# Splitting the loads of three early units into shares of partitions, in an instance norm on one core

## The chip, the core and the metric

The kernel runs on one core of one Trainium2 chip. The metric is the device time of one execution in microseconds (us). Before the change the median of three runs is 626.89 us (626.75 to 627.43). The core has five engines: TensorE (PE), VectorE (DVE), ScalarE (ACT), GpSimd (POOL) and SyncE (SP). Data moves between the main memory (HBM) and the on-chip memory (SBUF, 128 partitions) by 16 DMA engines. SP, ACT and POOL can start a transfer; SP and ACT each have a queue of their own, which the profile calls q1 (SP) and q10 (ACT). POOL's is q0.

## The reference

```
B, G, C_per_g, H, W = 4, 8, 16, 256, 256        # x, float32; gamma is (G, C_per_g)
mu  = x.mean(axis=(3, 4), keepdims=True)
var = ((x - mu) ** 2).mean(axis=(3, 4), keepdims=True)
out = (x - mu) / np.sqrt(var + 1e-5) * gamma[None, :, :, None, None]
```

For each of 4 x 8 x 16 = 512 images of 256 x 256 values the kernel takes the mean and the variance, normalizes, and multiplies by one factor per channel. Everything is float32. Each value has to be read once and written once: 134.2 MB in and 134.2 MB out.

## The kernel before, in words

**Tiling.** One image of 65,536 values is laid over S = 8 partitions, 8,192 values (32 KB) on each. So 16 images fill 128 partitions: this is a *unit*, 4 MB, and there are 32 units, numbered u = 0 to 31. Both `xv[u]` and `ov[u]` are 128 rows of 32 KB that lie one behind the other in HBM; row p of a unit goes to partition p. Partition p holds part p % 8 of image p // 8.

**Buffers.** Six SBUF buffers `slots[0..5]` (tiles `xt0` to `xt5`, in the profile `xt`), used in turn: unit u has slot u % 6. The normalization works in place, the store reads the slot, and the load of unit u + 6 can start when the store of unit u has landed.

**The order of the work** is the order in which the program is written (`manual_schedule`); the framework adds the waits. At the start, ahead of all computing:

- DVE clears a small tile `touch`, and POOL writes it (16 rows of 512 bytes) over the heads of every eighth row of unit 0 of the output (L54). The first store waits for that write. POOL also loads gamma (L55).
- Units 0 to 5 are loaded (L56, L57 through `load`, L47, L48): units 1 and 3 from ACT's queue, units 0, 2, 4 and 5 from SP's. Each is one transfer of 128 rows.
- L59 and L60 write 60 no-ops for ACT.
- Constants are made, among them the matrix `navg` that averages over the 8 partitions of an image, and gamma is brought to one value per partition (L83 to L94). ACT's first computing work is L78, a square root that needs its function table loaded.

Then one round for each unit u:

1. DVE sums each row of the slot (L107); beside it ACT squares it and sums the squares (L108, output thrown away).
2. TensorE multiplies the two sums by `navg` (L116); the result is minus the mean and minus the mean square.
3. DVE makes minus the variance (L117), ACT takes the root (L121), DVE the reciprocal (L125) and the product with gamma (L127).
4. DVE normalizes the slot in place (L130).
5. ACT issues the store (L134). SP issues the load of unit u + 6 (L136).

**Queues.** A queue works its transfers off in the order of issue. From unit 0 on, all stores are on ACT's queue (q10) and all further loads on SP's (q1). ACT and SP are in-order: an issue that has to wait holds up what stands behind it on that engine.

**Completion semaphores.** The transfers of SP and ACT share eight completion semaphores (numbers 99, 101, 112, 113, 114, 116, 117 and 118 in the trace). The framework deals them out in turn. An issue that gets a semaphore whose last transfer has not been seen to land waits for it first. In the program before, the six first loads and the first two stores use up the eight, so no load at the start waits.

Of the kernel before, what the change touches and what calls it, by code (L numbers as in the profile page):

```python
# [1 line left out]

# [4 lines left out]

F32 = mybir.dt.float32
U8 = mybir.dt.uint8
ALU = mybir.AluOpType  # L10
ACTF = mybir.ActivationFunctionType
AX = mybir.AxisListType


@with_exitstack
def kernel(
    ctx: ExitStack,
    tc: tile.TileContext,
    x: bass.AP,
    gamma: bass.AP,  # L20
    out: bass.AP,
):
    nc = tc.nc
    B, G, C, H, W = x.shape
    P = nc.NUM_PARTITIONS
    HW = H * W
    n_ch = B * G * C
    S = 8
    K = P // S
    F = HW // S  # L30
    U = n_ch // K
    NG = (G * C) // K
    AHEAD = 6
    assert HW % S == 0 and (G * C) % K == 0

    xv = x.rearrange("b g c h w -> (b g c h w)").rearrange("(u p f) -> u p f", p=P, f=F)
    ov = out.rearrange("b g c h w -> (b g c h w)").rearrange("(u p f) -> u p f", p=P, f=F)
    gv = gamma.rearrange("g c -> (g c)")

    data = ctx.enter_context(tc.tile_pool(name="data", bufs=1))  # L40
    singles = ctx.enter_context(tc.tile_pool(name="singles", bufs=1))
    psum = ctx.enter_context(tc.tile_pool(name="psum", bufs=4, space=bass.MemoryType.PSUM))
    ctx.enter_context(tc.manual_schedule())

    slots = [data.tile([P, F], F32, name=f"xt{i}") for i in range(AHEAD)]

    def load(u, queue):  # L47
        queue.dma_start(out=slots[u % AHEAD][:], in_=xv[u])  # L48


    g_row = singles.tile([1, G * C], F32, name="g_row")
    touch = singles.tile([16, 128], F32, name="touch")
    nc.vector.memset(touch[:], 0.0)  # L53
    nc.gpsimd.dma_start(out=ov[0][0::S, 0:128], in_=touch[:])  # L54
    nc.gpsimd.dma_start(out=g_row[:], in_=gv[None, :])  # L55
    for u in range(AHEAD):  # L56
        load(u, nc.scalar if u in (1, 3) else nc.sync)  # L57

    for _ in range(60):  # L59
        nc.scalar.nop()  # L60

    eps_t = singles.tile([P, 1], F32, name="eps_t")
    nc.gpsimd.memset(eps_t[:], 1e-5)
    one = singles.tile([1, 1], F32, name="one")
    nc.gpsimd.memset(one[:], 1.0)
    navg = singles.tile([P, K, S], F32, name="navg")
    nc.gpsimd.memset(navg[:], -1.0 / HW)  # L67
    nc.gpsimd.affine_select(  # L68
        out=navg[:], in_=navg[:], pattern=[[-S, K], [0, S]], compare_op=ALU.is_ge,
        fill=0.0, base=0, channel_multiplier=1,  # L70
    )
    nc.gpsimd.affine_select(  # L72
        out=navg[:], in_=navg[:], pattern=[[S, K], [0, S]], compare_op=ALU.is_ge,
        fill=0.0, base=S - 1, channel_multiplier=-1,
    )
    navg_w = navg[:].rearrange("p k s -> p (k s)")
    root_eps = singles.tile([P, 1], F32, name="root_eps")
    nc.scalar.activation(out=root_eps[:], in_=eps_t[:], func=ACTF.Sqrt)  # L78
    g_rep = singles.tile([1, NG, K, S], F32, name="g_rep")
    g_ps = psum.tile([P, NG], F32, name="g_ps", bufs=1)  # L80
    g_col = singles.tile([P, NG], F32, name="g_col")

    nc.vector.tensor_copy(  # L83
        out=g_rep[:],
        in_=g_row[:].rearrange("o (n k) -> o n k", n=NG).unsqueeze(3).to_broadcast([1, NG, K, S]),
    )
    for n in range(NG):
        nc.tensor.matmul(  # L88
            out=g_ps[:, n : n + 1],
            lhsT=g_rep[:, n].rearrange("o k s -> o (k s)"),  # L90
            rhs=one[:],
            start=True, stop=True,
        )
    nc.vector.tensor_copy(out=g_col[:], in_=g_ps[:])  # L94

    junk = singles.tile([P, F], U8, name="junk")

    st = singles.tile([P, U, 2], F32, name="st")
    nvar = singles.tile([P, U], F32, name="nvar")
    std = singles.tile([P, U], F32, name="std")  # L100
    rstd = singles.tile([P, U], F32, name="rstd")
    scale = singles.tile([P, U], F32, name="scale")

    squares = []
    for u in range(U):
        t = slots[u % AHEAD]
        nc.vector.reduce_sum(out=st[:, u, 0:1], in_=t[:], axis=AX.X)  # L107
        square = nc.scalar.activation(  # L108
            out=junk[:], in_=t[:], func=ACTF.Square, accum_out=st[:, u, 1:2],
        )  # L110
        if u:

            tc.declare_no_dep(square.ins, squares[-1].ins, reason="junk, ordered by the root between")
        squares.append(square)
        ps = psum.tile([P, 2], F32, name="ps")
        nc.tensor.matmul(out=ps[:], lhsT=navg_w, rhs=st[:, u], start=True, stop=True)  # L116
        nc.vector.tensor_scalar(  # L117
            out=nvar[:, u : u + 1], in0=ps[:, 0:1], scalar1=ps[:, 0:1],
            scalar2=ps[:, 1:2], op0=ALU.mult, op1=ALU.add,
        )  # L120
        nc.scalar.activation(  # L121
            out=std[:, u : u + 1], in_=nvar[:, u : u + 1], func=ACTF.Sqrt,
            bias=eps_t[:], scale=-1.0,
        )
        nc.vector.reciprocal(out=rstd[:, u : u + 1], in_=std[:, u : u + 1])  # L125
        g = u % NG
        nc.vector.tensor_mul(  # L127
            out=scale[:, u : u + 1], in0=rstd[:, u : u + 1], in1=g_col[:, g : g + 1],
        )
        nc.vector.tensor_scalar(  # L130
            out=t[:], in0=t[:], scalar1=ps[:, 0:1], scalar2=scale[:, u : u + 1],
            op0=ALU.add, op1=ALU.mult,
        )
        nc.scalar.dma_start(out=ov[u], in_=t[:])  # L134
        if u + AHEAD < U:
            load(u + AHEAD, nc.sync)  # L136


# [1 line left out]
_INS = ['x', 'gamma']  # L140
_OUTS = [((4, 8, 16, 256, 256), 'float32')]


# [23 lines left out]
```

## Time and profile before

| What | Value | From |
|---|---|---|
| time, median of 3 runs | 626.89 us (626.75 to 627.43) | runs |
| span of the profiled execution, its own time from the first to the last instruction | 624.9 us | page, head |
| DVE, ACT, PE, POOL busy | 443.4, 238.8, 21.4, 2.4 us | page, part 1 |
| bytes moved, mean rate over the span | 268.46 MB, 430 GB/s | page, part 2 |
| one load or store of a unit | 4096 KB | page, part 6 |
| from issue to landing, median: stores, SP's loads, ACT's two loads | 62.5, 38.5, 31.5 us | page, part 6 |
| row sum of a unit (DVE), squares (ACT), normalization (DVE) | 8685, 7030, 4550 ns | page, part 5 |
| instructions recorded on ACT | 98 | page, part 1 |

The page belongs to one profiled execution. The runs are timed without a profile; their median is 2.0 us above the span, which leaves that much around the first and the last instruction. In the page, part 2 cuts the span into 40 equal slices of 15.62 us; a digit is the busy share in tenths. The rate row below it says what the 16 DMA engines together moved in each slice.

Besides the page, the trace holds one record for every packet of every transfer: its queue, start, duration and size. A packet here is one row of 32,768 bytes; a packet of 4 bytes is the signal to a completion semaphore, one per DMA engine and transfer. There are 8,192 packets of 32,768 bytes: 512 for each of the 16 DMA engines.

### The profile page before, as it was taken

The page shows a single profiled execution, that of the slowest core. Times are in us where ns is not written, and L with a number is a line of the kernel's source. Part 1 is how long each engine was busy: PE and PEld are TensorE (multiplying, and loading weights), DVE is VectorE, ACT ScalarE, POOL GpSimd, SP SyncE. Part 2 cuts the span into 40 slices and gives each one's busy share as a digit, 9 for nine tenths or more (in the row PEclk, how much of TensorE's full clock was granted, in tenths as well). Part 3 has the DMA queues.
Part 4 walks back from the last instruction along what each step waited for, and adds up shares of the span by engine and source line. Part 5 has one row for each costly group of instructions (what it writes and reads, how often), then busy time and mean ns, then how long its engine had stood idle before and what let it go on. Part 6 is the DMA issues. An engine that isn't in the chain of part 4 may idle for free.

```text
span 624.9 us, 631 instructions
## 1 busy us (share of the span) xinstructions
PE 21.4 (3%) x80; PEld 19.5 (3%) x80; DVE 443.4 (71%) x163; ACT 238.8 (38%) x98; POOL 2.4 (0%) x11
## 2 busy tenths in 40 slices
PE   0200000000000000000000000000000000000000
PEld 0200000000000000000000000000000000000000
DVE  0588999999776687666786767867668676687730
ACT  0444444444443234432344423444224442244400
POOL 1000000000000000000000000000000000000000
DMA  8999999999999999999999999999999999999998
GB/s 370 436 426 430 422 434 436 436 436 437 432 424 433 436 436 424 436 436 434 436 436 432 422 436 436 434 426 436 436 434 436 436 434 419 436 436 434 426 436 369
DMA packets 9282, 268.46 MB, mean 430 GB/s; under 512 B 1072, under 2 KB 1088, under 8 KB 1088
## 3 DMA queue, kind: packets, MB, share of 16 engines
q10 hardware_dynamic: 4896, 142.61, 52.9%
q1 hardware_dynamic: 4320, 125.83, 46.8%
q0 software_dynamic: 64, 0.01, 0.0%
q14 instruction: 2, 0.02, 0.0%
HBM read 134.22 MB, written 134.23 MB: 430 GB/s over the span
## 4 chain that ended last, share of the span: by engine, by line
another core or an unknown queue 61%; DMA 17%; DVE 15%; SPq 1%; PE 1%; issue 0%; ACT 0%
DVE st L107 10%; DMA xt<-in_x_dram 10%; DMA out_dram<-xt 8%; DVE xt L130 5%; SPq L48 1%; PE ps L116 1%; ACT std L121 0%; DVE nvar L117 0%; DVE rstd L125 0%; DVE scale L127 0%
## 5 line engine op out<-in xcount | busy, mean ns | idle before, releaser
L107 DVE TENSOR_REDUCE st<-xt 128x1 f32<-128x8192 f32 x32 | 277.9, 8685 | 100.4 <-DMA xt<-in_x_dram 100.4
L108 ACT ACTIVATE junk<-xt 128x8192 uint8<-128x8192 f32 x32 | 225.0, 7030 | 275.1 <-DMA xt<-in_x_dram 231.9
L130 DVE TENSOR_SCALAR xt<-xt,ps,scale 128x8192 f32<-128x8192 f32 x32 | 145.6, 4550 | 1.2
L121 ACT ACTIVATE std<-nvar,eps_t 128x1 f32<-128x1 f32 x32 | 9.4, 294 | 79.6 <-DVE nvar L117 79.6
L116 PE MATMUL ps<-st,navg 128*128 128x2 f32 x64 | 17.9, 349 | 557.1 <-DVE st L107 557.1
L116 PEld LDWEIGHTS ps<-st,navg 128*128 128x128 f32 x64 | 16.0, 311 | 558.9 <-issue 558.9
L117 DVE TENSOR_SCALAR nvar<-ps 128x1 f32<-128x1 f32 x32 | 9.2, 287 | 23.8 <-PE ps L116 23.8
L125 DVE RECIPROCAL rstd<-std 128x1 f32<-128x1 f32 x32 | 5.2, 164 | 11.6 <-ACT std L121 11.6
L83 DVE COPY g_rep<-g_row 1x1024 f32<-1x1024 f32 x1 | 0.7, 681 | 14.3 <-DMA g_row<-in_gamma_dram 14.3
L108 ACT ACTIVATION_READ_ACCUMULATOR junk<-xt 128x1 f32 x32 | 6.0, 186 | 0.0
L127 DVE TENSOR_TENSOR scale<-rstd,g_col 128x1 f32<-128x1 f32 x32 | 5.1, 159 | 1.1
L88 PE MATMUL g_ps<-one,g_rep 1*128 1x1 f32 x16 | 3.5, 347 | 16.1 <-DVE g_rep L83 16.1
L88 PEld LDWEIGHTS g_ps<-one,g_rep 1*128 1x128 f32 x16 | 3.5, 325 | 16.1 <-issue 16.1
L94 DVE COPY g_col<-g_ps 128x8 f32<-128x8 f32 x1 | 0.2, 166 | 3.7 <-PE g_ps L88 3.7
L78 ACT ACT_TABLE_LOAD x1 | 1.3, 1283 | 1.7 <-PEq L151 1.7
L53 DVE MEMSET touch<- 16x128 f32 x1 | 0.2, 165 | 0.9 <-PEq L151 0.9
L54 POOL DMA_DIRECT2D out_dram<-touch x1 | 0.6, 619 | 0.8 <-DVE touch L53 0.8
L55 POOL DMA_DIRECT2D g_row<-in_gamma_dram x1 | 0.5, 487 | 0.0
L68 POOL TENSOR_SCALAR_AFFINE_SELECT navg<-navg 128x128 f32<-128x128 f32 x1 | 0.4, 400 | 0.1
L72 POOL TENSOR_SCALAR_AFFINE_SELECT navg<-navg 128x128 f32<-128x128 f32 x1 | 0.4, 399 | 0.1
L67 POOL MEMSET navg<- 128x128 f32 x1 | 0.2, 232 | 0.0
L78 ACT ACTIVATE root_eps<-eps_t 128x1 f32<-128x1 f32 x1 | 0.2, 203 | 0.0
(6 smaller groups left out, 0.6 us busy)
## 6 DMA issues: line engine op xcount, KB each, us to landing
out_dram<-xt ACTq DMA_DIRECT2D x32, 4096.0 KB, 62.5
xt<-in_x_dram SPq DMA_DIRECT2D x30, 4096.0 KB, 38.5
xt<-in_x_dram ACTq DMA_DIRECT2D x2, 4096.0 KB, 31.5
out_dram<-touch POOLq DMA_DIRECT2D x1, 8.0 KB, 9.1
g_row<-in_gamma_dram POOLq DMA_DIRECT2D x1, 0.5 KB, 13.3
```

Source lines behind the costliest of these rows:

```text
L48: queue.dma_start(out=slots[u % AHEAD][:], in_=xv[u])
L78: nc.scalar.activation(out=root_eps[:], in_=eps_t[:], func=ACTF.Sqrt)
L83: nc.vector.tensor_copy(out=g_rep[:], in_=g_row[:].rearrange("o (n k) -> o n k", n=NG).unsqueeze(3).to_broadcast([1, NG, K, S]),)
L88: nc.tensor.matmul(out=g_ps[:, n : n + 1], lhsT=g_rep[:, n].rearrange("o k s -> o (k s)"), rhs=one[:], start=True, stop=True,)
L107: nc.vector.reduce_sum(out=st[:, u, 0:1], in_=t[:], axis=AX.X)
L108: square = nc.scalar.activation(out=junk[:], in_=t[:], func=ACTF.Square, accum_out=st[:, u, 1:2],)
L116: nc.tensor.matmul(out=ps[:], lhsT=navg_w, rhs=st[:, u], start=True, stop=True)
L117: nc.vector.tensor_scalar(out=nvar[:, u : u + 1], in0=ps[:, 0:1], scalar1=ps[:, 0:1], scalar2=ps[:, 1:2], op0=ALU.mult, op1=ALU.add,)
L121: nc.scalar.activation(out=std[:, u : u + 1], in_=nvar[:, u : u + 1], func=ACTF.Sqrt, bias=eps_t[:], scale=-1.0,)
L125: nc.vector.reciprocal(out=rstd[:, u : u + 1], in_=std[:, u : u + 1])
L127: nc.vector.tensor_mul(out=scale[:, u : u + 1], in0=rstd[:, u : u + 1], in1=g_col[:, g : g + 1],)
L130: nc.vector.tensor_scalar(out=t[:], in0=t[:], scalar1=ps[:, 0:1], scalar2=scale[:, u : u + 1], op0=ALU.add, op1=ALU.mult,)
```

## The change

`load` cuts the first use of three slots into several transfers. A share is written as (first, step): partitions first, first + step, first + 2 step and so on, with the rows of the unit in HBM that belong to them.

- Units 2 and 3: (0, 8) and (4, 8) with 16 rows each, (2, 4) with 32 rows, (1, 2) with 64 rows.
- Unit 4: (0, 4) and (2, 4) with 32 rows each, (1, 2) with 64 rows.
- All other units stay one transfer of 128 rows. The 64 large transfers become 72.
- The loop of 60 no-ops is taken out of the source.

```
+    shares = {
+        2: ((0, S), (S // 2, S), (S // 4, S // 2), (1, 2)),
+        3: ((0, S), (S // 2, S), (S // 4, S // 2), (1, 2)),
+        4: ((0, S // 2), (S // 4, S // 2), (1, 2)),
+    }
+
     def load(u, queue):
-        queue.dma_start(out=slots[u % AHEAD][:], in_=xv[u])
+        for first, step in shares.get(u, ((0, 1),)):
+            queue.dma_start(out=slots[u % AHEAD][first::step], in_=xv[u][first::step])
...
     for u in range(AHEAD):
         load(u, nc.scalar if u in (1, 3) else nc.sync)
-
-    for _ in range(60):
-        nc.scalar.nop()
```

With more transfers at the start, the eight completion semaphores come round sooner, and the built program has waits at these issues that it did not have before:

- SP: the fourth share of unit 2 waits until unit 0 has landed; the three shares of unit 4 wait for the first share of unit 3 and the first and second of unit 2; unit 5 waits for the third share of unit 3.
- ACT: the fourth share of unit 3 waits until unit 1 has landed. ACT's function table (L78 before, L83 after) stands behind it.
- The stores of units 0, 1 and 2 wait for the second share of unit 3, the third of unit 2 and the first of unit 4; the stores of units 4 and 5 for the loads of units 5 and 6.

From unit 6 on, the transfers are the same as before and in the same order; the semaphores fall back into the old rotation.

## The prediction, made before the changed kernel was run

> **What bounds the kernel now.** I read the page's head and parts 2 and 3 first, to see which resource is full.
>
> ```profile
> span 624.9 us, 631 instructions
> ...
> DMA  8999999999999999999999999999999999999998
> GB/s 370 436 426 430 422 434 436 436 436 437 432 424 433 436 436 424 436 436 434 436 436 432 422 436 436 434 426 436 436 434 436 436 434 419 436 436 434 426 436 369
> DMA packets 9282, 268.46 MB, mean 430 GB/s; under 512 B 1072, under 2 KB 1088, under 8 KB 1088
> ...
> q10 hardware_dynamic: 4896, 142.61, 52.9%
> q1 hardware_dynamic: 4320, 125.83, 46.8%
> ```
>
> The DMA engines are busy in every slice, and the rate stops at 436 to 437 GB/s. The two queues together take 99.7% of the engines' span. So the compute engines matter only if they leave the queues without work. Then the chain of waits, in the steady part:
>
> ```profile
> 159.95 18.96 another core or an unknown queue
> 178.91 0.02 SPq L48
> 178.93 0.03 issue
> 178.96 0.33 SPq L48
> 179.29 18.95 another core or an unknown queue
> 198.25 0.02 SPq L48
> ```
>
> SP issues one load per 198.25 - 178.91 = 19.34 us, each time a store has landed. In that time each DMA engine moves 8 rows of a load and 8 of a store: 19.34 / 16 = 1.21 us per row. The trace's packet records say the same: 98% of the 8,192 rows take 1.213 us, none under 1.211, on both queues alike. The floor is then 512 x 1.213 = 621.06 us of rows per engine. The first row starts at 1.80 us and the last signal is at 623.61; the floor would end at 622.86. Only 0.75 us are lost over the whole kernel, and 1.3 us follow.
>
> How much room have the waits? The timeline of the start:
>
> ```profile
> 0.80 0.88 ACTq L48 DMA_DIRECT2D xt<-in_x_dram  x2
> ...
> 1.72 1.28 ACT L78 ACT_TABLE_LOAD   x1 [1.72 <-PEq L151]
> ...
> 3.01 0.20 ACT L78 ACTIVATE root_eps<-eps_t 128x1 f32<-128x1 f32 x1
> ...
> 22.62 7.03 ACT L108 ACTIVATE junk<-xt 128x8192 uint8<-128x8192 f32 x1 [19.41 <-DMA xt<-in_x_dram]
> 22.62 8.69 DVE L107 TENSOR_REDUCE st<-xt 128x1 f32<-128x8192 f32 x1 [2.73 <-DMA xt<-in_x_dram]
> 29.56 0.19 ACT L108 ACTIVATION_READ_ACCUMULATOR junk<-xt 128x1 f32 x1
> 31.42 0.50 PEld L116 LDWEIGHTS ps<-st,navg 128*128 128x128 f32 x2 [11.82 <-issue]
> ...
> 37.68 0.35 ACTq L134 DMA_DIRECT2D out_dram<-xt  x1
> ```
>
> ACT's issues end at 1.68 and its table load starts at 1.72: the 60 no-ops take no time between them and the trace has no record of one. Units 0 and 1 land at 22.25 (records), units 2 and 3 at 41.7; store 0 is issued 3.6 us ahead of that (41.26, when the first engine turns to it).
>
> **The change, part by part.**
>
> *No-ops.* Nothing on the chip goes away: 0 us.
>
> *More signals.* Eight more transfers put eight more 4-byte packets on each DMA engine. In the records one takes 0.009 us, and the next packet starts 6 ns later: 8 x 0.006 to 0.009 = 0.05 to 0.07 us. I take 0.05. All of it is on the path, for nothing covers the full resource. The rows themselves stay 512 per engine if a share of 16 rows gives one to each engine; the 16 rows of `touch` did so (16 records that start between 7.12 and 7.69, one behind a row of each engine).
>
> *ACT's new wait.* ACT sits until unit 1 has landed, wakes at 22.62 (as its squares did), issues the fourth share of unit 3 (0.4, from 0.88 for 2), loads its table (1.28) and takes L78's root (0.20). The squares of unit 0 begin at about 24.5, not 22.62, and end at 31.5, READ_ACCUMULATOR at 31.75. TensorE started at 31.42, just after DVE's sum. Unit 0 and its store come 0.4 us later: 38.1. Cover: units 2 and 3 keep the engines until 41.26, 3 us to spare. DVE carries the 0.4 on to unit 8 (its round of 14.93 us gains on the 19.34 of the loads until then), always with a store waiting in the queue. Cost 0; if the cover were gone, 0.4.
>
> *SP's new waits.* The fourth share of unit 2 is issued at 22.6 and needed at 21.7 + 8 rows x 1.213 = 31.4 (four rows of each queue go ahead). Unit 4 then waits for shares that land by 31, unit 5 for unit 3's third share, by 31 to 37; they are needed at 41 and 61. The next in SP, load 6, waits for store 0 (61.8) as now. Room 8 us or more each: 0.
>
> *The stores' new waits.* Store 0 waits for a share that lands by 27 (ready 38), store 1 by 37 (ready 53), store 2 by 52 (ready 68), stores 4 and 5 for loads 5 and 6, at about 81 and 100 (ready 98 and 113). Each is done 10 us early or more, and still 5 us early if the loads come 4.85 later: 0.
>
> *The shares of 16 rows.* No row of this trace prices them: every large transfer in it has 128 rows. Each engine gets four rows of this kind (two first shares, two second shares). Below: 0, each stays at 1.213; a gain is excluded by the 1.211 minimum. Above: two engines meet at the same part of SBUF and share one engine's rate, 2 x 1.213 per row, 4 x 1.213 = +4.85 us. Which? The row time is 1.213 where both queues load (units 2 and 3, 22 to 38 us) and where loads run beside stores (from 44 us on), for reading HBM and for writing it. Such a ceiling belongs to the DMA engine or to its way into SBUF. A whole load has all 128 partitions, so no engine need meet another; a share (0, 8) uses every eighth partition only, and if neighbours share a way, some ways get two engines and others none. The second share uses the idle ones, but a queue comes to it only later, and units 2 and 3 go through the same shares side by side, so the other queue gives no relief. I take the upper end, less a little: two engines out of step by s do not meet for s at each end. The starts of the 16 engines lie 0.57 us apart (21.67 to 22.24), and the closest pair sets the end: s about 0.1, 0.2 off. +4.65 us.
>
> The Trainium skill, page "SBUF — State Buffer", section "Door 1: The DMA port swizzle", gives a map by which partitions 0, 8, 16 ... 120 reach eight of 16 ports, two rows each, and 4, 12 ... 124 the other eight; it puts a port at one engine's rate, so a 16-row share would go at half speed: an estimate of +4.85 for the term, against 0 if the rows stay at the trace's 1.213. No run here shows it yet.
>
> *The shares of 32 and 64 rows.* Below 0, above 1.213 more on each of the other 20 rows per engine (2 + 4 of unit 2, 2 + 4 of unit 3, 2 + 2 + 4 of unit 4): +24.3. I take 0: step 4 and step 2 still touch every group of four neighbours, as a whole load does, with two and four rows per engine.
>
> **Sum.** 0.05 + 0 + 4.65 = 4.7 us. The profiled execution's span goes from 624.9 to 629.6; with the 2.0 us around it (626.89 - 624.9) the time is 631.6. Nothing gives it back, since the rows run to the end: the last store is issued at 600.3 and then waits in the queue until 623.6.
>
> **Rivals.**
>
> *The limit is in the engine, not on the way into SBUF* (not slower). Place: the first two shares of units 2 and 3, 21.7 to 31.4. It decides if a way carries two engines at once; then only the signals are left: 626.9 + 0.05 = 626.9. For it: each DMA engine alone explains the 1.213. Against it: nothing in the trace, which never makes two engines meet. Chance 0.26, the small shifts by instruction fetches (two records of 8 KB at 155.6 and 199.1, 0.3 us each on one engine) within it.
>
> *The wide shares collide too*, all 24 split rows of an engine: 626.9 + 4.85 + 24.3 = 656. It needs rows of a wide share to be dealt out otherwise than in a whole load. Chance 0.04.
>
> *A queue runs dry behind a wait* that lands late, which needs 3 us (store 0) or 8 us (the loads) more than worked out, on both queues at once. It would cost a few us on top: 634 to 637. Chance 0.03.
>
> *Faster.* What is lost now is 0.75 us, so 626.1 at best; over 0.2% (1.25 us) faster needs what the floor excludes. 0.02, for an error in my reading.
>
> **How the numbers follow.** The likeliest case has 0.65: 631.6, its own range 630.5 to 632.3 (from pairs 0.5 us out of step, 626.9 + 3.9 with 0.3 of noise off, to 626.9 + 4.85 + 0.07 with 0.5 of noise on; the runs spread 0.68). For 8 in 10 the engine rival must be inside: 626.4 to 632.4, leaving out 656, the dry queue and the faster case. 0.2% is 1.25 us, about what a measurement of this kernel tells from no change. Slower 0.65 + 0.04 + 0.03 = 0.72, the same 0.26, faster 0.02.
>
> **What would show it.** In the records of units 2 and 3: 64 rows of about 2.4 us on 16 engines between 21.7 and 31.4 and nowhere else; the rate row's slices 2 and 3 (15.6 to 46.9) fall, with about 218 GB/s in the 9.7 us from 21.7. Load 2 lands near 46.4, store 0 starts moving then, and everything after is 4.7 us later. ACT's table load stands near 23, store 0's issue near 38.1. I am wrong if these rows stay at 1.213 (time 626.9), if rows of wide shares double, or if slices after 47 us fall below 436.

## The result, and the profile after

The changed kernel takes 632.19 us (631.64 to 632.54), the one before 626.95 us on the same footing. The ratio is 1.0081, with a 95% interval of 1.0068 to 1.0093: 5.2 us slower. The forecast was 631.6, slower by 4.7.

The head, part 2 and the packet count of the page of the changed kernel:

```profile
span 630.1 us, 648 instructions
...
DMA  8999999999999999999999999999999999999997
GB/s 367 316 416 433 433 433 433 433 433 431 433 433 433 433 433 433 433 433 433 435 433 435 433 435 433 437 435 433 437 433 433 433 435 437 435 435 435 433 433 339
DMA packets 9410, 268.47 MB, mean 426 GB/s; under 512 B 1200, under 2 KB 1216, under 8 KB 1216
```

The DMA engines stay busy in every slice, so no queue ran dry. But the second slice (15.75 to 31.5 us) moves 316 GB/s instead of 436. After it the rate is back. The busy share and the rate part here: the engines hold rows longer without moving more. The 1,200 small packets are 128 more than before, 8 per DMA engine, one for each added transfer.

Windows of the same two stretches, first of the kernel before, then of the changed one. The last column is GB/s, the one before it the DMA busy share:

```profile
21.60:31.40 9.80, 0.00 (x0) 0.00 (x0) 8.69 (x1) 7.12 (x2) 0.00 (x0) 1.00 1.00 431
31.40:41.00 9.60, 0.56 (x2) 0.50 (x2) 8.51 (x5) 3.22 (x2) 0.00 (x0) 1.00 1.02 433
...
62.00:600.00 538.00, 16.18 (x58) 14.53 (x58) 405.81 (x149) 215.38 (x88) 0.00 (x0) 1.00 1.00 433
```

```profile
21.60:31.40 9.80, 0.00 (x0) 0.00 (x0) 8.38 (x1) 7.56 (x3) 0.00 (x0) 1.00 1.04 231
31.40:41.00 9.60, 0.56 (x2) 0.50 (x2) 7.84 (x6) 3.17 (x4) 0.00 (x0) 1.00 1.00 420
...
62.00:600.00 538.00, 16.16 (x58) 14.52 (x58) 400.93 (x146) 215.09 (x87) 0.00 (x0) 1.00 1.00 434
```

Nearly the whole loss lies where the four shares of 16 rows move. From 62 us on the two kernels run at the same rate.

The packet records say it row by row. Each DMA engine moves the rows of units 2 and 3 in turn, one from q1, one from q10. The mean time of the k-th row over the 16 engines, in us (my grouping of the records; row 1 and 2 are the two 16-row shares, 3 and 4 the share of 32, 5 to 8 the share of 64, and on q1 "next" is the first row of unit 4):

```
                    row 1   2     3     4     5 to 8   next
before  q1 (unit 2) 1.21  1.21  1.21  1.21    1.21     1.74
        q10 (unit 3) 1.21 1.21  1.21  1.21  1.21, last 1.33
after   q1          2.06  2.31  1.68  1.22    1.22     1.22
        q10         2.57  2.57  1.21  1.22    1.22     1.21
```

The timeline of the start, after (L83 is the table load and root that were L78, L113 the squares, L139 the store):

```profile
23.02 8.69 DVE L112 TENSOR_REDUCE st<-xt 128x1 f32<-128x8192 f32 x1 [3.13 <-DMA xt<-in_x_dram]
23.83 1.28 ACT L83 ACT_TABLE_LOAD   x1 [23.83 <-DMA xt<-in_x_dram]
25.12 0.20 ACT L83 ACTIVATE root_eps<-eps_t 128x1 f32<-128x1 f32 x1
25.23 7.01 ACT L113 ACTIVATE junk<-xt 128x8192 uint8<-128x8192 f32 x1
...
38.66 0.36 ACTq L139 DMA_DIRECT2D out_dram<-xt  x1
```

ACT's table load has moved from 1.72 to 23.83, behind the wait for unit 1, and the first store from 37.68 to 38.66. Its first row starts at 47.6 (43.0 before), so that costs nothing.

**Where the 5.2 us come from**, per DMA engine and from the records: the slow rows of units 2 and 3 are 5.13 us over 1.213 each (0.85 + 1.36 + 1.10 + 1.36 + 0.47). The slow rows at 40 to 43 us of the kernel before (1.74 and 1.33 in the table) are gone: -0.64. The 4-byte signals take 0.70 instead of 0.59: +0.11. That makes 4.60; the mean end of the 16 engines moves from 623.08 to 627.66, by 4.58. The last engine ends 1.03 behind that mean instead of 0.53: +0.50. The stretch from the last signal to the end is 0.1 longer. Together 5.2, the difference of the spans (630.1 - 624.9).

### The profile page after: what moved, and what is told of

It reads as the page before. It is cut to its first block, busy times and chain, and to the rows that moved or that the text cites. A ratio compares the mean times of both kernels' runs of the same rounds, so it can differ in the third digit from the quotient of the medians.

```text
span 630.1 us, 648 instructions
## 1 busy us (share of the span) xinstructions
PE 21.4 (3%) x80; PEld 19.5 (3%) x80; DVE 443.5 (70%) x163; ACT 238.7 (38%) x98; POOL 2.4 (0%) x11
## 4 chain that ended last, share of the span: by engine, by line
another core or an unknown queue 60%; DMA 18%; DVE 12%; issue 2%; ACT 2%; SPq 1%; PE 1%; ACTq 0%; DVEq 0%
DMA xt<-in_x_dram 10%; DVE st L112 8%; DMA out_dram<-xt 8%; DVE xt L135 3%; SPq L56 1%; ACT junk L113 1%; PE ps L121 1%; ACT std L126 0%; DVE nvar L122 0%; ACT L83 0%; DVE rstd L130 0%; DVE scale L132 0%; ACTq L56 0%; ACT root_eps L83 0%
## 5 line engine op out<-in xcount | busy, mean ns | idle before, releaser
L113 ACT ACTIVATE junk<-xt 128x8192 uint8<-128x8192 f32 x32 | 224.9, 7029 | 260.8 <-DMA xt<-in_x_dram 222.8
L113 ACT ACTIVATION_READ_ACCUMULATOR junk<-xt 128x1 f32 x32 | 6.0, 186 | 0.0
L83 ACT ACTIVATE root_eps<-eps_t 128x1 f32<-128x1 f32 x1 | 0.2, 202 | 0.0
```

Of the source, the lines that this page charges most:

```text
L113: square = nc.scalar.activation(out=junk[:], in_=t[:], func=ACTF.Square, accum_out=st[:, u, 1:2],)
```

## The experiments

**Theory.** In a share of 16 rows two DMA engines meet at one part of SBUF, because of the partitions it reaches. **Rivals**: the number of transfers with their signals and waits; small shares as such, or the distance of their rows in HBM; both queues being in the same share. In the diffs a share is (first, step) where nothing else is said. Runs 1 to 7 edit the changed kernel, runs 8 to 12 the kernel before, without its no-ops; the diffs show the lines that matter. No record names the part of SBUF that an engine writes; that engines meet there is read from the times of the rows.

**1. No share of 16 rows, nearly as many transfers.**

```
-        2: ((0, S), (S // 2, S), (S // 4, S // 2), (1, 2)),
-        3: ((0, S), (S // 2, S), (S // 4, S // 2), (1, 2)),
+        2: ((0, S // 2), (S // 4, S // 2), (1, 2)),
+        3: ((0, S // 2), (S // 4, S // 2), (1, 2)),
```

> Units 2, 3 and 4 all in the three shares that unit 4 has (32, 32 and 64 rows), so no share of 16 rows; 70 large transfers instead of 72, nearly the same new waits. Theory (two DMA engines meet at one part of SBUF in the 16-row shares): all rows stay at 1.213 us, the time falls back to 627.0 (between 626.3 and 627.4). Rival (the number of transfers and their waits cost the time): 6 of the 8 extra transfers are left, so about 6/8 of the 5.2 us stays, 630.8.

Measured: 627.84 us against 627.02, ratio 1.0010 (1.0001 to 1.0019). No row of units 2 and 3 is over 1.22, except the last of unit 3 (1.50 on average; one of the slow rows at 41 us that the kernel before has too). So the count of transfers and the new waits are not what costs; 0.8 us stay, a little over the range I gave. Of these the mean end of the engines explains 0.2 (623.29 against 623.08), the last engine 0.6 more (624.38 against 623.61).

**2. Only unit 2 in four shares.**

```
-        3: ((0, S), (S // 2, S), (S // 4, S // 2), (1, 2)),
-        4: ((0, S // 2), (S // 4, S // 2), (1, 2)),
```

> Only unit 2 is split in the four shares; units 3 and 4 are whole. Theory: two rows per DMA engine instead of four take twice as long, so half of the rows' surplus of 5.1 us: +2.4 to +2.6, 629.4. The rows of unit 3, which run between them on the other queue, stay at 1.213. Rival (it needs both queues in the same shares at the same time): 627.0. Rival (count of transfers, 3 of 8): 628.9, with no doubled rows.

Measured: 629.99 us, ratio 1.0044 (1.0030 to 1.0057), about 3 us of the 5.2. It does not need both queues in the same share. But the rows of unit 3 did not stay at 1.213: unit 2's first two rows take 2.07 and 2.15, and unit 3's first and third row 1.68 and 1.58, together 2.6 over. A whole load that runs beside a contested share loses too.

**3 and 4. Halves: blocks of 64 partitions, or even and odd.** Unit 4 is whole in both. Count, size and waits are the same.

```
+        2: ((0, 64), (64, 128)),        # from, to
+        3: ((0, 64), (64, 128)),
```

> Units 2 and 3 in two halves each, partitions 0 to 63 and 64 to 127; two extra transfers only, no share under 64 rows and no new wait of a load. Theory (what counts is which partitions a transfer reaches at one time): a half that is a block of partitions has two engines at one part of SBUF, so all 16 rows per engine of units 2 and 3 take about 2.4 us: +19 us, 646. Rival (small shares of 16 rows are slow in themselves, or the number of transfers): no loss, 627.

```
+        2: ((0, 2), (1, 2)),
+        3: ((0, 2), (1, 2)),
```

> The same count and size of shares as the kernel with blocks of 64, but the halves are even and odd partitions. Theory: all rows stay at 1.213 us, 627.0 (626.3 to 627.4). Rival (any transfer of fewer than 128 rows is slower): as slow as the halves in blocks, 646.

Measured: blocks 648.14 us, ratio 1.0334 (1.0319 to 1.0350); even and odd 627.42 us, ratio 1.0005 (0.9996 to 1.0014). Windows, first of the blocks, then of even and odd:

```profile
21.60:31.40 9.80, 0.00 (x0) 0.00 (x0) 8.20 (x1) 7.12 (x2) 0.00 (x0) 1.00 1.04 221
31.40:41.00 9.60, 0.56 (x2) 0.50 (x2) 8.42 (x6) 2.63 (x2) 0.00 (x0) 1.00 1.03 212
41.00:62.00 21.00, 0.56 (x2) 0.50 (x2) 10.99 (x5) 5.08 (x3) 0.00 (x0) 1.00 0.98 203
62.00:600.00 538.00, 16.17 (x58) 14.53 (x58) 399.33 (x145) 215.09 (x87) 0.00 (x0) 1.00 1.00 433
```

```profile
21.60:31.40 9.80, 0.00 (x0) 0.00 (x0) 8.69 (x1) 7.12 (x2) 0.00 (x0) 1.00 0.99 428
31.40:41.00 9.60, 0.56 (x2) 0.50 (x2) 8.51 (x5) 3.20 (x2) 0.00 (x0) 1.00 1.02 437
41.00:62.00 21.00, 1.12 (x4) 1.01 (x4) 19.08 (x7) 11.63 (x5) 0.00 (x0) 1.00 1.01 424
```

This is the pair that decides. Two transfers of 64 rows each, and the whole difference is which partitions are in a half, with the rows of HBM that belong to them (run 5 takes these two apart). In blocks nearly every row of units 2 and 3 takes 2.56 us and the rate is half for 40 us; even and odd partitions leave the rows at 1.21. Small shares are not slow in themselves, and a large one can be.

The Trainium skill, page "SBUF — State Buffer", section "Door 1: The DMA port swizzle", says that partitions 0 to 63 reach only 8 of 16 ports. The traces agree in the rate: 203 to 221 GB/s in blocks, 428 to 437 with even and odd.

**5. The partitions of the change, the rows of HBM in blocks.**

```
+        row = 0
         for first, step in shares.get(u, ((0, 1),)):
-            queue.dma_start(out=slots[u % AHEAD][first::step], in_=xv[u][first::step])
+            n = P // step if step < S else P // S
+            queue.dma_start(out=slots[u % AHEAD][first::step], in_=xv[u][row : row + n])
+            row += n
```

> The shares, the partitions and the waits of the change, but each share reads rows that lie one behind the other in HBM (rows 0 to 15, 16 to 31 and so on) instead of every eighth. Units 2, 3 and 4 so have rows of other images in their partitions, and their output is not the reference's; the work is the same. Theory (the partitions in SBUF decide): the same 64 rows of 2.1 to 2.6 us, 632.2. Rival (sixteen rows 256 KB apart in HBM are slow to read): 627.0.

Measured: 632.10 us, ratio 1.0080 (1.0066 to 1.0093), as the change itself. Its window:

```profile
21.60:31.40 9.80, 0.00 (x0) 0.00 (x0) 8.33 (x1) 7.48 (x3) 0.00 (x0) 1.00 1.05 234
```

The same hole. The distance of the rows in HBM has no part in it.

**6. Only unit 4 split.**

```
-        2: ((0, S), (S // 2, S), (S // 4, S // 2), (1, 2)),
-        3: ((0, S), (S // 2, S), (S // 4, S // 2), (1, 2)),
```

> Only unit 4 is split, in its three shares; units 2 and 3 are whole. For the main theory nothing: all rows stay at 1.213 us, 627.0 (626.3 to 627.6). For the 0.6 us that rows lose at 41 us before the change and not after it: if the late issue of unit 4 takes that loss away, it is gone here (time 626.4); if it is the lead of the first store over its turn in the queue (3.6 us here as before), the slow rows at 41 us are still there.

Measured: 627.68 us, ratio 1.0010 (1.0001 to 1.0018), a little over the upper edge that I gave. The rows stay at 1.213, the slow rows at 41 us are there (16 of 1.73). So the late issue of unit 4 is not what took them away in the changed kernel.

**7. Unit 2 in blocks of 16, 16, 32 and 64 partitions.**

```
+        2: ((0, 16), (16, 32), (32, 64), (64, 128)),     # from, to; units 3 and 4 whole
```

> Only unit 2 is split, in blocks of partitions: 0 to 15, 16 to 31, 32 to 63, 64 to 127. Theory (engines share a part of SBUF, four neighbours to a part): in the 16-row blocks four DMA engines meet, these rows take four times 1.213, about 4.9 us; in the blocks of 32 and 64 rows two meet, about 2.5 us. Surplus 2 x 3.7 + 6 x 1.3 = 15.2 us, 642. Rival (a transfer of 16 rows runs at half rate, wherever its rows go, and two is the most that meet): 8 x 1.3 = 10.4 us, 637.

Measured: 643.89 us, ratio 1.0263 (1.0247 to 1.0278); 642 was expected, 637 by the rival. The rows of the two 16-row blocks take 3.77 and 3.87 us on average, up to 4.62, those of the 32 and 64 rows 2.0 to 2.6. Read by the theory, more than two engines meet there. It is not a fixed rate for 16 rows: the same number of rows takes 2.1 to 2.6 in the change and 3.8 here. That the time came so near 642 is partly luck: the rows of unit 2 lose 11.8 us per engine and not 15.2 (a 16-row block was put at 4.9 us per row), and the whole rows of unit 3 beside them, which the sum left out, lose 5.5.

**8. Units 0 and 1 one after the other, each by parity over both queues.** This began as a try at the 0.6 us of slow rows at 41 us, and at a kernel faster than both.

```
     for u in range(AHEAD):
-        load(u, nc.scalar if u in (1, 3) else nc.sync)
+        if u < 2:
+            nc.sync.dma_start(out=slots[u][0::2], in_=xv[u][0::2])
+            nc.scalar.dma_start(out=slots[u][1::2], in_=xv[u][1::2])
+        else:
+            load(u, nc.scalar if u == 3 else nc.sync)
```

> The kernel before, but units 0 and 1 come one after the other: each as even partitions from SP's queue and odd partitions from ACT's. Unit 0 lands at about 12 us instead of 22, and the first store is issued at about 35 (gamma holds DVE until 20) instead of 37.7; its turn in the queue stays at 41.3. Theory for the 0.6 us (the first store needs more than 3.6 us of lead): the slow rows at 41 us vanish, 626.4, the first version that would be faster than before. Rival (the loss belongs to the first store as such, or to unit 4's first row): still there, 627.0.

Measured: 644.48 us, ratio 1.0275 (1.0261 to 1.0289). Neither theory had that. Its page:

```profile
GB/s 360 449 400 434 443 424 420 424 425 432 426 420 423 424 426 424 426 414 428 418 432 426 422 422 416 430 428 416 424 418 432 420 422 424 416 426 422 430 441 198
```

The slow rows that it was to remove are there as well (the first two rows of unit 4 take 1.40 and 1.83 on average). No hole, but a rate of about 424 throughout, and 198 in the last slice. By the records, ten pairs of units take 198.5 us instead of 193.6, with rows of 1.4 to 2.1 us where the units change, and the 16 engines end between 629.4 and 641.0, while before they end within 0.9 us. One thing differs from the start: SP's queue moved two rows before ACT's moved one, so a unit on q10 ends 2.4 us after its partner on q1. The last four runs looked into that.

**9 to 12. A lead for SP's queue, all loads whole.** ACT loads its table and takes its root ahead of its two loads (9); in 10 its constant comes later, in 11 and 12 DVE makes it behind two or three clears of a scratch tile.

```
+    eps_t = singles.tile([P, 1], F32, name="eps_t")
+    nc.gpsimd.memset(eps_t[:], 1e-5)            # 11 and 12: pause cleared 2 or 3 times, then this, on nc.vector
+    root_eps = singles.tile([P, 1], F32, name="root_eps")
+    nc.scalar.activation(out=root_eps[:], in_=eps_t[:], func=ACTF.Sqrt)
     for u in range(AHEAD):
         load(u, nc.scalar if u in (1, 3) else nc.sync)
```

> The kernel before with all loads whole, but ACT loads its function table and takes the root ahead of its two loads, so that its queue starts about 1.5 us later. Question: in the run with units 0 and 1 by parity, SP's queue was one row ahead (a unit on q10 ended 2.4 us after its partner on q1 instead of together), and from 62 us on a pair of units took 19.85 us instead of 19.36. If that lead of one row is the cause, and ACT's queue here also misses one row, the same slow pairs come back: 640 to 645. If the parity halves of units 0 and 1 were the cause, or if the lead is no whole row here: 627.0.

> The same, with ACT's constant written later, so that its queue starts about 2.5 us late: a lead of one or two rows for SP's queue. If a lead of one row is what is slow and here it is one: 640 to 645; if any lead is slow, two rows as well; if two rows are harmless, as in the run with blocks of 16 (partners 5 us apart, pairs of 19.37 us): 627.0 to 628.

> All loads whole; ACT's constant is made by DVE behind two short clears of a scratch tile, so that ACT issues its loads at about 1.7 us, between 0.94 (where SP's queue had no lead) and 2.61 (three rows of lead). Aim: a lead of exactly one row. If a lead of one row is what slows the steady part, partners end 2.4 us apart and pairs take 19.85 us: 640 to 645. If one row is harmless, as three were: 627.0, and what was slow in the run with units 0 and 1 by parity stays open.

> The same with three clears, ACT's loads at about 2.0 us: a lead of one or two rows. One row: as above, 640 to 645 or 627.0. Two rows: 627.0 to 628, as two and three rows were harmless so far.

Measured: 626.96, 627.03, 627.03 and 627.14 us, ratios 0.9999 (0.9985 to 1.0013), 0.9999 (0.9985 to 1.0013), 1.0002 (0.9993 to 1.0012) and 1.0003 (0.9993 to 1.0013). The lead was none in 9, three rows on most engines in 10, two in 11, and two on most engines in 12 (the signals of partners are 0, 6.5, 4.8 and 5.4 us apart on the mean of the engines). The timeline of 9 shows why it had none:

```profile
0.80 1.28 ACT L54 ACT_TABLE_LOAD   x1 [0.80 <-PEq L148]
...
0.81 1.92 SPq L48 DMA_DIRECT2D xt<-in_x_dram  x4
...
0.94 0.86 ACTq L48 DMA_DIRECT2D xt<-in_x_dram  x2
```

ACT issued its loads 0.14 us after the table load had begun, not behind it. So leads of two and three rows are harmless. No run with whole loads has given SP's queue a lead of one row. The other way round it stands in the changed kernel and in runs 1, 5 and 6: from the load of unit 5 on, the store on q10 ends 2.4 us ahead of the load beside it on q1, and ten such pairs take 193.7 to 193.8 us, against 193.6 before. So one row out of step is not slow in that direction; whether it is in the other, or the parity halves made run 8 slow, stays open. Run 10 also ends the theory on the slow rows at 41 us: its first store is issued at 35.35 and its first row starts at 45.5, a lead of 10 us, and the slow rows are there (two of q1's rows on each engine, 1.50 and 1.72 on average).

## Why the prediction was right

- *The bound.* Right: the rows run to the end and nothing gives a lost microsecond back. The rate after 62 us is 433 and 434. But the floor was set too high. The records of two rows that follow each other on one engine overlap by 4 ns: in the kernel before, the next row starts 1.209 us after the last one (median), not 1.213. So 512 rows need 619.0 us and not 621.06, and the mean engine lost 2.3 us (623.08 - 1.80 - 619.0), not 0.75. The bound stands, but "626.1 at best", on which the small chance of a faster kernel rested, does not.
- *No-ops, 0.* Right as far as shown: neither trace has one. The table load that followed at once before now waits for a load, which the no-ops have nothing to do with.
- *Signals, +0.05.* Measured 0.11 per engine. Some signals next to contested rows take 0.01 to 0.03 instead of 0.009.
- *ACT's wait, 0.* The cost was right, the size was not: the store comes 1.0 us later, not 0.4. I let ACT wake 0.4 us after the last signal as before; it woke 0.7 later than that (the issue is at 23.30 against 22.62). The cover was 7.7 us in the end (46.39, when the first engine is done with unit 3, less 38.66).
- *SP's and the stores' waits, 0.* Right. Run 1 has nearly all of them and none of the contested rows.
- *16-row shares, +4.65.* The mechanism is shown by runs 3, 4 and 5: the partitions of a share decide, not its size, not HBM. The size was off: 5.13 us, above the upper end of 4.85. I had bounded a contested row by twice 1.213 = 2.43; where two engines meet throughout it is 2.56 to 2.57, and one engine's contest runs on into the row behind (1.68). What I took off for engines out of step, 0.2, shows only in the two rows of q1 (2.06 and 2.31), and the row behind them (1.68) takes more than half of it back.
- *32 and 64 rows, 0.* Right: 1.22 in the change, and run 1.
- *What the sum left out.* The slow rows at 41 us that vanish (-0.64) and the last engine (+0.50). That these two nearly cancel is luck: so the sum is 0.5 us short, no more than the term for the 16-row shares is by itself. I had put the first into the 0.75 us "lost" and let it stand.
- *The rivals.* A limit in the engine alone is refuted by run 3, wide shares that collide by run 4. That the trace of before "never makes two engines meet" was the right reason not to trust its flat 1.213.
- *What would show it.* 64 rows of about 2.4 between 21.7 and 31.4: they are 64 with means of 2.06 to 2.57, plus 16 behind them (1.68) that I did not name. The rate there is 231 GB/s (218 expected), the last engine's signal of load 2 is at 46.8 (46.4). One sign of being wrong was badly set: most slices after 47 us are below 436 (433 in many), but so were many of the kernel before, and the rate after 62 us is the same in both.

## What to carry to other kernels

In these runs a load into SBUF kept its full rate when the partitions that its 16 engines work on at one moment were spread as those of a whole 128-row load are: even and odd halves, or every fourth row with 32 rows, kept 1.21 us per row, while blocks of 64 or every eighth row with 16 rows took double, and blocks of 16 about three times as long. In a kernel whose DMA engines are never idle, look at time per row and not at the busy share, for a contested engine is as busy as a working one. The slow rows also slow whole loads on the other queue, and every microsecond of it arrives at the end.

## What the runs showed of the hardware that was not expected

- Two engines that meet lose more than half: 2.56 us per row instead of 2.43 (median of the 256 split rows of run 3).
- The slow rows at 41 us, 0.6 to 0.9 us per engine, around the first store's turn in the queue. They are there in the kernel before and in runs 1, 4, 6 and 8 to 12, and absent in the change and in runs 2 and 5, where units 2 and 3 had contested rows. The issue of unit 4 and the lead of the first store were excluded (runs 6 and 10). The cause is open.
- Run 8: two queues one row out of step, or halves by parity ahead of everything, cost 17 us: the mean engine ends 11.8 us later, through rows of 1.4 to 2.1 us where the units change, and the last engine 6.1 us behind that mean. Leads of two and three rows, and one row the other way round, cost nothing. The cause is open.
- The last engine's distance to the mean end differs between kernels (0.5 before, 1.0 in the change, 1.1 in run 1, 0.85 in run 6) and shows up in the time. In each trace two records of 8 KB for instructions delay a row each by 0.3 us and make the row behind them 0.25 to 0.65 longer. In the kernel before, the last engine is one of these. In the change and in runs 1 and 6 it is another, which falls back in small steps (in run 1 the engine with the record ends at 623.9, the last at 624.4); why is open.
